# A fused matmul, tanh and multiply: pair blocks with 7 products replaced by triple blocks with 15

## The chip, the cores and the metric

The kernel runs on one core of one Trainium2 chip. The metric is device microseconds (us) for one execution, lower is better. The core has five engines that run their own instruction streams and meet through semaphores: TensorE (PE, matmuls; PEld is its weight load), VectorE (DVE), ScalarE (ACT), GpSimd (POOL) and SyncE (SP), which here only issues DMAs. Matmul results land in PSUM, eight banks of 128 partitions by 512 float32 numbers; all other on-chip data lie in SBUF.

## The reference

```python
x:  16 x 512 x 1024   float32, normal numbers
w1: 1024 x 768, w2: 1024 x 768   float32, normal numbers
y1 = np.matmul(x, w1)
y2 = np.matmul(x, w2)
return (np.tanh(y1) * y2).astype(np.float32)
```

Flattened, x is 8192 rows, that is 64 row tiles of 128 rows. The contraction length is 1024, eight blocks of 128. The output is 8192 by 768.

## The kernel before

**Head.** The first six row tiles (HEAD = 6) are computed plainly, in bfloat16, while the weights still arrive: x and the weights are loaded by SP (`load_head_x`, `load_w`), cast on DVE and ACT (`cast_wb`, L254 and L256), x is transposed on PE (`pe_transpose_f` L223 for tiles 0 to 3, `pe_transpose_b` L238 for tiles 4 and 5), and `head_mm` multiplies: 512 columns wide (L267) and 256 wide (L270), eight contraction blocks each, for both weights. `head_tanh` (L283) and `head_mul` (L287) finish, `head_store` stores. Meanwhile the sums of absolute values of the weights (`abs_w` L260), `sum_w_all` (L300) and `powers` (L347 to L350) give a power of two for each weight, with which DVE and ACT make scaled float16 blocks `b11`, `b21`, `b22` (`cast_w`) and their differences `t1` to `t4` (`t_block`, L318 and L322).

**Steady part.** The other 58 row tiles go in 29 pairs. A pair of tiles (two block rows) by the two halves of the contraction, against the two halves of the contraction by the two halves of a weight's columns, is a 2x2 by 2x2 block product, done with 7 block products in place of 8 by the scheme that the names s1 to s4, t1 to t4 and p1 to p7 spell out. A *unit* is one pair with one weight: 7 products, each four matmuls of 384 columns (`product`, L401). The combinations after the products are made in part by accumulating several products in one PSUM bank, in part by ACT copies (`op_seed` L414 seeds a bank with another's contents, `copy_out` L418), in part by DVE additions (`add_out` L423). For w1 the unit ends with tanh on ACT with a scale (L431), for w2 with a multiplication on DVE (`final`, L437) into the output tile, which SP stores (L452).

**Operands of x.** For each pair: SP loads two tiles (L334), ACT sums absolute values (L340), DVE takes powers of two (L347 to L350), DVE or ACT casts with the reciprocal to float16 (L360, L362), SP transposes by DMA (L368), DVE makes four operand sums of 128x512 (L382), and `out_scales` (L390) prepares the factors that undo the scaling.

**Order.** The first ten units and the head follow ORDER, four lists written out (PE, ACT, DVE, DMA); `schedule` gives them times with cost figures and emits them in that order. Later units follow a fixed slot table: seven slots of 0.65 us a unit, with a due slot for each step (`unit_ops`). Products stand in the slots -6 p1, -3 p5, -2 p2, 0 p6, 2 p3, 3 p7, 6 p4. The steps on ACT and DVE that hand a bank on lie between: p7 (slot 3), then the DVE addition c22, then p4 (slot 6). Neighbouring units overlap and fill each other's gaps. GpSimd issues nothing in the steady part; it does four small steps for the last two units (L442, L448).

**The end.** The last multiplication on DVE covers 384 columns, and its store 192 KB; the other halves of the last tiles were stored earlier.

Of the kernel before, what the change touches and what calls it, by code (L numbers as in the profile page):

```python
# [8 lines left out]
ACT = mybir.ActivationFunctionType  # L9
ALU = mybir.AluOpType  # L10


@with_exitstack
def kernel(
# [15 lines left out]

    nc = tc.nc
# [3 lines left out]
    BM = B * M  # L35
    KO = K // P
    KH = KO // 2
    MT = BM // P
    Q = N // 2
    F = 512  # L40
    G = N - F
    HEAD = 6
    WARM = 21
    PAIRS = (MT - HEAD) // 2
    FIRST = 6
    PLANNED = 10
    T_BUFS = 2
    O_BUFS = 4
    LOADS = ("x0 a0 x1 a1 x2 a2 x3 a3 a4 a5 a6 a7 b0 b1 b2 b3 b4 b5 b6 b7").split()
    ABS = ((1, 1, 1, 1, 1, 1, 1, 1), (2, 0, 2, 0, 2, 0, 1, 1))  # L50
    GATE = {4: 2, 5: 4, 6: 6, 7: 7}
    BLOCKS = ({"b11": ("dve", 20), "t1": ("dve", 22), "b22": ("act", 23), "t2": ("dve", 25), "b21": ("act", 25),
               "t3": ("dve", 28), "t4": ("dve", 30)},
              {"b11": ("act", 42), "t1": ("dve", 44), "b22": ("act", 46), "t2": ("dve", 48), "b21": ("act", 45),
               "t3": ("dve", 50), "t4": ("dve", 52)})
    EARLY = ("La0", "La1", "La2", "La3")

    ELSEWHERE = {
        "e01": "dve", "e11": "dve", "e20": "act", "e21": "dve", "e31": "dve", "ca0": "act", "ca1": "act",
        "cb4": "act", "b22a": "dve", "cx11": "act", "cx31": "act", "cx61": "act"  # L60
    }
    FILL = {"m00F0": 3, "m00F1": 6}
    ORDER = {
        "pe": """
            T00 T01 m00F0 m00G0 T10 T11 m00F1 m00G1 m10F0 T20 m10G0 m10G1 m10F1 T21 m20G0 m20F0 m20F1 m20G1
            m10G2 m20G2 m00F2 m00G2 m20F2 m10F2 T30 T31 m10G3 m00G3 m20F3 m10F3 m20G3 m00F3 m10F4 m10G4 m20F4
            m20G4 m00G4 m00F4 m30G0 m30G1 m30G2 m30G3 m20G5 m10G5 m10F5 m20F5 m20G6 m10G6 m10F6 m30G4 m30G5
            m30G6 m20G7 m10G7 m30G7 m10F7 m00F5 m00F6 m00F7 suma m11F0 m20F6 m20F7 m01F0 m00G5 m00G6 m00G7
            m11F1 m01F1 m30F0 m30F1 m30F2 m30F3 m30F4 m30F5 m30F6 m30F7 m21F0 m21F1 m11F2 m21F2 m01F2 m11F3
            m21F3 m01F3 m31F0 m31F1 m31F2 m31F3 m21G0 m21G1 m21G2 m21G3 m31G0 m31G1 m31G2 m31G3 m01F4 m31G4  # L70
            m21G4 m11F4 m01G0 m01G1 m11G0 m11G1 m01G2 m01G3 m01G4 m31F4 T4 m11F5 m11F6 m01F5 m31F5 m01G5 m01G6
            m31F6 m01F6 m31G5 m31G6 m01F7 m31F7 m11F7 m31G7 T5 m40F0 m40F1 m40F2 m40F3 m40F4 m40F5 m40F6 m01G7
            m40F7 m21G5 m21G6 m50F0 m50F1 m50F2 m50F3 m50F4 m50F5 m50F6 m50F7 m21F4 m21F5 m21G7 m21F6 m21F7
            m11G2 m11G3 m11G4 m11G5 m11G6 m11G7 m40G0 m50G0 m50G1 m50G2 m50G3 m50G4 m50G5 m50G6 m50G7 m40G1
            m40G2 m40G3 m40G4 m40G5 m40G6 m40G7 sumb m41F0 m41F1 m41F2 m41F3 m41F4 m41F5 m41F6 m41F7 m41G0
            m41G1 m41G2 m41G3 m41G4 m41G5 m41G6 m51G0 m51G1 m51G2 m51G3 m51G4 m51G5 m51G6 m51G7 m41G7 m51F0
            m51F1 m51F2 m51F3 m51F4 m51F5 m51F6 m51F7 p1.0 p1.1 p5.0 p6.0 p2.0 p3.0 p7.0 p5.1 p6.1 p4.0 p2.1
            p7.1 p1.2 p3.1 p4.1 p1.3 p6.2 p2.2 p5.2 p6.3 p2.3 p5.3 p7.2 p7.3 p3.2 p4.2 p3.3 p4.3 p1.4 p1.5
            p5.4 p5.5 p2.4 p6.4 p6.5 p2.5 p7.4 p7.5 p3.4 p3.5 p4.4 p4.5 p1.6 p1.7 p5.6 p6.6 p2.6 p6.7 p2.7
            p7.6 p3.6 p5.7 p7.7 p4.6 p3.7 p1.8 p4.7 p1.9 p2.8 p6.8 p5.8 p5.9 p7.8 p1.10 p3.8 p4.8 p3.9 p6.9  # L80
            p2.9 p2.10 p7.9 p5.10 p4.9
        """,
        "act": """
            ca0 absa0 ca1 absa1 e20 absa2 absa3 absa4 absa5 absa6 absa7 tanh2G absb0 tanh1F tanh0G tanh2F cb4
            tanh0F absb2 absb6 tanh3F absb4 ax00 absb7 ax01 b21a tanh4F tanh5F ax10 ax11 tanh4G ax20 cx11 b11b
            b22b seed.0 seed.1 s5.0 u2.0 ax21 b21b u2.1 f00.0 s5.1 f10.0 ax31 seed.2 ax30 seed.3 f11.0 u2.2
            u2.3 s5.2 s5.3 f00.2 f01.0 ax40 cx31 f10.2 seed.4 ax41 seed.5 s5.4 s5.5 u2.4 u2.5 f11.2 f00.4 ax51
            f01.2 ax50 f10.4 seed.6 f11.4 seed.7 f01.4 u2.6 s5.6 ax61 u2.7 s5.7 f00.6 f11.6 f10.6 seed.8 ax60
            f00.8 u2.8 f01.6 s5.8 cx61 s5.9 seed.9 f10.8 seed.10 u2.9 f01.8 f11.8 f00.10 s5.10
        """,  # L90
        "dve": """
            e00 e01 e10 e11 ca2 e21 ca3 ca4 e30 ca5 ca6 e31 ca7 parta cb0 cb1 scalea b11a cb2 cb3 t1a b22a hx4
            cb6 cb5 t2a e41 cb7 hx5 mul0F mul3F mul1F e51 t3a rx0 cx00 cx01 mul2G mul2F mul0G partb t4a rx1
            cx10 scaleb mul4F sx0 mul4G s1.0 s2.0 s4.0 s3.0 sx1 t1b t2b t3b c22.0 rx2 sx2 cx20 t4b s1.1 c22.1
            f00.1 s2.1 c12.0 f10.1 s3.1 cx21 c12.1 s4.1 f11.1 rx3 cx30 c22.2 c22.3 s3.2 s1.2 f00.3 f01.1 c12.2
            c12.3 s2.2 f10.3 mul5F rx4 cx40 s4.2 cx41 s3.3 c22.4 f11.3 c22.5 f00.5 s1.3 c12.4 f01.3 s2.3 f10.5
            rx5 f11.5 s4.3 cx50 c12.5 f01.5 c22.6 sx3 cx51 c22.7 f00.7 s1.4 s2.4 sx4 s3.4 c12.6 c12.7 rx6 cx60
            s4.4 sx5 f01.7 c22.8 f10.7 f11.7 s1.5 s2.5 c12.8 s3.5 c12.9 f00.9 c22.9 s4.5 f11.9 f01.9 f10.9
        """,
        "dma": """  # L100
            Lx0 La0 Lx1 La1 Lx2 La2 Lx3 La3 La4 La5 La6 La7 Lb0 Lb1 Lb2 Lb3 Lb4 Lx4 Lb5 Lb6 Lx5 Lb7 Lp00 Lp01
            Lp10 Lp11 Tx00 Lp20 Tx01 st3 Lp21 Tx10 Lp30 st4 Tx11 Lp31 st1 Tx20 Lp40 Lp41 Tx21 st2 Lp50 Tx30
            Lp51 Tx31 Lp60 st5 Tx40 Lp61 st0 Tx41 Lp70 store1.5 Tx50 store0.5 Lp71 Tx51 store0.1 store1.1 Tx60
            store0.7 store1.7 Tx61 store1.3 store0.3 store0.9 store1.9
        """,
    }
    LATENCY = {"pe": 0.2, "act": 0.12, "dve": 0.12, "dma": 1.4, "pool": 1.4, "none": 0.0}

    bf16 = mybir.dt.bfloat16
    f16 = mybir.dt.float16  # L110
    f32 = mybir.dt.float32
    i32 = mybir.dt.int32
# [5 lines left out]
    pool = lambda name, bufs: ctx.enter_context(tc.tile_pool(name=name, bufs=bufs))  # L118
    once = pool("once", 1)
    xfpool = pool("xf", 6)  # L120
    xhpool = pool("xh", 4)
    xtpool = pool("xt", 10)
    spool = pool("s", 3)
    smpool = pool("sm", 8)
    hopool = pool("ho", HEAD // 2)
    pspool = ctx.enter_context(tc.tile_pool(name="ps", bufs=1, space=bass.MemoryType.PSUM))
    banks = [pspool.tile([P, 512], f32, name=f"bank{i}") for i in range(8)]

    pin = tc.keep_in_program_order

    head_stack, opool = ExitStack(), []
    head = head_stack.enter_context(tc.tile_pool(name="head", bufs=1))
    w1_stack = ExitStack()
    w1_pool = w1_stack.enter_context(tc.tile_pool(name="w1f", bufs=1, side="right"))
    w_f = [p.tile([P, KO, N], f32, name=f"wf{t}") for t, p in enumerate((w1_pool, head))]
    w_b = [[head.tile([P, N], bf16, name=f"wb{t}{k}") for k in range(KO)] for t in range(2)]
    asum_w = [once.tile([P, sum(n > 0 for n in ABS[t])], f32, name=f"asum_w{t}") for t in range(2)]
    junk = once.tile([P, 2 * N], bf16, name="junk")  # L140
    ones = once.tile([P, P], f32, name="ones")
    ident = once.tile([P, P], f32, name="ident")
    ident_b = once.tile([P, P], bf16, name="ident_b")

    wt = [{n: once.tile([P, KH, Q], f16, name=f"{n}_{t}")
           for n in ("b11", "b21", "b22", "t1", "t2", "t3", "t4")}
          for t in range(2)]

    def feed(n, bank=banks[3]):
        for _ in range(n):
            pin(nc.tensor.matmul(bank[:, :2 * P], ones.bitcast(bf16)[:, :P], ones.bitcast(bf16), start=True, stop=True))

    pin(nc.vector.memset(ones, 2.0 ** -12))
    feed(WARM, banks[7])
    make_identity(nc, ident)
    pin(nc.vector.tensor_copy(ident_b, ident))

    events = []

    def at(time, fn, *args):
        events.append((time, len(events), fn, args))

    def emit():
        for _, _, fn, args in sorted(events, key=lambda e: e[:2]):
            fn(*args)
        events.clear()  # L170

    plan = {}

    def op(name, engine, cost, due, needs, fn, *args):
        plan[name] = (engine, cost, [n for n in needs if n], fn, args)
# [576 lines left out]
```

## Time and profile before

The runs took 316.24 to 316.66 us, median 316.66. The profiled execution has a span of 314.2 us from the first to the last instruction; so 2.46 us lie between this span and the median, outside the instructions that the profile shows.

| From the profile before | Value |
|---|---|
| Span of the profiled execution, beside the median | 314.2 us, 316.66 us |
| Granted PE clock | 1.000 |
| First matmul that is not a warm-up, first product of a unit, last product | 6.2, 43.9, ends about 310.5 us |
| HBM read, written | 39.85 MB, 25.17 MB |
| DMA queue of SP and ACT, share of 16 engines | 88.0% |
| x loads: count, size, issue to landing | 64, 512 KB, 5.8 us |
| DMA transposes: count, issue to landing | 58, 3.7 us |
| Stores of 384 KB: count, issue to landing | 62, 3.6 us |
| Stores of 192 KB from SP: count, issue to landing | 3, 1.9 us |

The profile's lines name the kernel's line, the engine, the operation, the tile written and those read, the shape and the number of instructions. "Busy" is the time in which an engine executed something. The chain of waits follows the work that ended last back to what released it, step by step, so it tells which engine the end depends on. A stretch's row lists each engine's busy time in it.

### The profile page before, as it was taken

How to read it: one execution, taken by the hardware profiler on the slowest of the kernel's cores; microseconds unless marked ns; L12 is line 12 of the kernel's file. 1: busy time of each engine (PE TensorE's matmuls, PEld its weight loads, DVE VectorE, ACT ScalarE, POOL GpSimd, SP SyncE). 2: the span in 40 equal slices, each digit the busy share in tenths (PEclk: the TensorE clock that was granted, in tenths of full speed). 3: DMA queues.
4: the chain of work that ended last, by engine and by line, in shares of the span. 5: the costliest groups of instructions: out<-in, count | busy, mean ns of one | idle time of the engine just before them, and what ended most of it. 6: DMA issues, size and time to landing. Idle time of an engine off the chain costs nothing.

```text
span 314.2 us, 5489 instructions
## 1 busy us (share of the span) xinstructions
PE 307.3 (98%) x1893; PEld 185.6 (59%) x1898; DVE 244.8 (78%) x571; ACT 230.5 (73%) x453; POOL 4.3 (1%) x10
## 2 busy tenths in 40 slices
PE   7999999999999999999999999999999999999995
PEld 5756656666656555555555556555555555555662
DVE  1688988888788778877777887777788777778653
ACT  3798879787888777778777777877777787776552
POOL 0000000000000000000000000000000000000004
PEclk9999999999999999999999999999999999999999
DMA  7999398999999999999999989999998989985322
GB/s 276 407 399 381 78 310 237 271 299 258 290 288 310 297 272 231 228 294 266 285 240 252 273 253 225 291 252 259 253 251 281 260 256 271 237 256 126 144 103 100
DMA packets 82300, 80.59 MB, mean 256 GB/s; under 512 B 63584, under 2 KB 64096, under 8 KB 82272
## 3 DMA queue, kind: packets, MB, share of 16 engines
q1 hardware_dynamic: 81552, 78.46, 88.0%
q10 hardware_dynamic: 720, 1.77, 1.4%
q8 instruction: 15, 0.25, 0.3%
q14 instruction: 13, 0.11, 0.1%
HBM read 39.85 MB, written 25.17 MB: 207 GB/s over the span
## 4 chain that ended last, share of the span: by engine, by line
PE 89%; DMA 8%; DVE 1%; issue 1%; ACT 0%; ACTq 0%; SPq 0%; DVEq 0%
PE bank L401 84%; DMA wf<-in_w_dram 8%; PE bank L267 3%; PE bank L270 2%; DVE t L318 1%; DVE s L382 1%; PE bank L238 0%; DVE o L437 0%; ACT o L283 0%; ACTq L250 0%; SPq L250 0%; ACT junk L260 0%; PE bank L300 0%; DVE o L287 0%; DVE out_r L390 0%
## 5 line engine op out<-in xcount | busy, mean ns | idle before, releaser
L401 PE MATMUL bank<-t,s 128*128 128x384 f16 x696 | 131.5, 326 | 0.4 <-DVE t L318 0.4
L401 PEld LDWEIGHTS <-s 128*128 128x128 f16 x928 | 90.7, 98 | 61.1 <-issue 0.8
L401 PEld LDWEIGHTS <-xT 128*128 128x128 f16 x696 | 68.0, 98 | 46.7 <-issue 0.9
L401 PE MATMUL bank<-b,xT 128*128 128x384 f16 x464 | 93.7, 326 | 0.0
L423 DVE TENSOR_TENSOR c<-bank,u 128x384 f32<-128x384 f32 x58 | 31.9, 553 | 41.1 <-PE bank L401 39.6
L340 ACT ACTIVATE junk<-x_f 128x1024 bf16<-128x1024 f32 x58 | 60.8, 1049 | 2.4 <-DMA x_f<-in_x_dram 2.4
L431 ACT ACTIVATE th<-c,out_r 128x384 f32<-128x384 f32 x58 | 35.3, 609 | 21.1 <-DVE c L423 21.1
L401 PE MATMUL bank<-b,s 128*128 128x384 f16 x232 | 47.0, 326 | 0.0
L401 PE MATMUL bank<-t,xT 128*128 128x384 f16 x232 | 46.9, 325 | 0.0
L418 ACT ACTIVATE u<-bank 128x384 f32<-128x384 f32 x58 | 28.2, 487 | 20.0 <-PE bank L401 19.7
L360 DVE TENSOR_SCALAR x_h<-x_f,pr 128x1024 f16<-128x1024 f32 x55 | 41.0, 746 | 0.2
L431 ACT ACTIVATE th<-bank,out_r 128x384 f32<-128x384 f32 x58 | 33.3, 574 | 6.1 <-PE bank L401 6.1
L414 ACT ACTIVATE bank<-bank 128x384 f32<-128x384 f32 x58 | 27.9, 481 | 12.6 <-DVE o L437 10.0
L437 DVE SCALAR_TENSOR_TENSOR o<-bank,out_r,th 128x384 f32<-128x384 f32 x58 | 35.4, 610 | 2.0 <-PE bank L401 2.0
L423 DVE TENSOR_TENSOR c<-bank,s 128x384 f32<-128x384 f32 x58 | 32.1, 554 | 6.1 <-PE bank L401 5.0
L437 DVE SCALAR_TENSOR_TENSOR o<-c,out_r,th 128x384 f32<-128x384 f32 (+1 forms) x57 | 34.3, 606 | 0.4 <-ACT th L431 0.2
L418 ACT ACTIVATE s<-bank 128x384 f32<-128x384 f32 x58 | 27.9, 482 | 7.3 <-PE bank L401 5.1
L382 DVE TENSOR_TENSOR s<-xT 128x512 f16<-128x512 f16 x58 | 24.0, 416 | 0.2
L267 PE MATMUL bank<-wb,xTb 128*128 128x512 bf16 x91 | 23.6, 379 | 0.1
L270 PE MATMUL bank<-wb,xTb 128*128 128x256 bf16 x96 | 14.6, 273 | 0.1
L260 ACT ACTIVATE junk<-wf 128x768 bf16<-128x768 f32 (+1 forms) x13 | 12.8, 988 | 1.4 <-DMA wf<-in_w_dram 1.2
L267 PEld LDWEIGHTS <-xTb 128*128 128x128 bf16 x96 | 9.3, 99 | 7.5 <-DVE xTb L231 0.3
(49 smaller groups left out, 143.4 us busy)
## 6 DMA issues: line engine op xcount, KB each, us to landing
x_f<-in_x_dram SPq DMA_DIRECT2D x64, 512.0 KB, 5.8
out_dram<-o SPq DMA_DIRECT2D x62, 384.0 KB, 3.6
wf<-in_w_dram SPq DMA_DIRECT2D x12, 384.0 KB, 7.7
wf<-in_w_dram ACTq DMA_DIRECT2D x4, 384.0 KB, 8.5
xT<-x_h SPq DMA_TRANSPOSE x58, 3.7
out_dram<-o SPq DMA_DIRECT2D x3, 192.0 KB, 1.9
out_dram<-o ACTq DMA_DIRECT2D x1, 192.0 KB, 1.9
```

Of the source, the lines that this page charges most:

```text
L260: pin(nc.scalar.activation(junk[:, :n * N].rearrange("p (k n) -> p k n", n=N), w_f[t][:, k:k + n, :], ACT.Abs, accum_out=asum_w[t][:, j:j ...
L267: pin(nc.tensor.matmul(bank, hx[mt][:, k, :], w_b[t][k][:, :F], start=k == 0, stop=k == KO - 1))
L270: pin(nc.tensor.matmul(bank[:, at_:at_ + G], hx[mt][:, k, :], w_b[t][k][:, F:], start=k == 0 and mt % 2 == 0, stop=k == KO - 1, skip_group ...
L340: pin(nc.scalar.activation(junk[:, :K], xs[HEAD + 2 * i + h], ACT.Abs, scale=2.0 ** -12, accum_out=pair_sum[i][:, h:h + 1]))
L360: pin(nc.vector.tensor_scalar(xh, xs.pop(mt), pair_r[i][:, h:h + 1], None, ALU.mult))
L382: pin((nc.vector if eng == "dve" else nc.gpsimd).tensor_tensor(s, st[i, a], st[i, b], op))
L401: pin(nc.tensor.matmul(bank[:, cols], st[i, a][:, k, :], wt[t][b][:, k, cols], start=start and k == 0, stop=stop and k == KH - 1, skip_gro ...
L414: pin(nc.scalar.activation(ub[u]["b"][:, :Q], ub[u]["a"][:, :Q], ACT.Copy))
L418: pin(nc.scalar.activation(c, ub[u][bank][:, :Q], ACT.Copy))
L423: pin(nc.vector.tensor_tensor(c, ub[u][bank][:, :Q], ub[u][other], ALU.add))
L431: pin(nc.scalar.activation(th, v, ACT.Tanh, scale=rs[i][:, 0, h:h + 1]))
L437: pin(nc.vector.scalar_tensor_tensor(o[:, h, q * Q + cols.start:q * Q + cols.stop], v, rs[i][:, 1, h:h + 1], tanhs[i, h, q][:, cols], ALU. ...
```

## The change

The head stays at six plain tiles, one plain tile is added at the end (TAIL = 1), and the other 57 go in 19 triples. In a triple, three row tiles by the two halves of the contraction meet two halves of the contraction by three column groups: columns 0 to 511 of w1, columns 0 to 511 of w2, and the last 256 columns of both weights side by side. Each group is 512 columns wide. The plain way takes 3 x 2 x 3 = 18 block products; the new scheme takes 15, p0 to p14, each four matmuls of 512 columns. Both weights are so done in one unit.

What it asks for beside the products: 11 sums of weight blocks, once (B_SUMS, DVE, 128x2048 float16 each); 10 sums of x blocks in each triple (A_SUMS, 128x512, on DVE or GpSimd); and in each triple 7 copies from PSUM on ACT ("copy", "seed"), 8 additions on DVE ("add"), three tanh and three multiplications of 512 columns ("t", "m") and of 256 ("th", "mh").

Operands are cast to float16 without scaling. The loads of tiles 4 to 63 convert from float32 in the DMA, issued from GpSimd; the transposes of these tiles are DMAs from SP. ACT still sums the absolute values of every x tile and of each of the 16 weight slices (`aw`), but nothing waits for them before the end. There, DVE and one matmul count how many of the sums lie between 512 and 1024 and write a flag; all engines load it into a register, and if a sum was outside, a branch takes `general_path`, which computes everything again with scaled operands, tile by tile.

The order of all engines' work is made by a class `Planner` when the kernel is built. It takes each step's needs, cost and due time, walks forward in time and gives each step to the engine, among those allowed, that can start it first. The order of the products is fixed by PE_ORDER, in which "+" marks products of the triple before. Its 15 positions give this table for one triple (in slots of one product): p10 0, p7 2, p6 4, p9 5, p12 7, p8 8, p11 10, p3 11, p4 16, p2 18, p13 21, p5 24, p1 27, p0 28, p14 29. PSUM banks are also given out by the planner.

```diff
-    HEAD = 6
-    PAIRS = (MT - HEAD) // 2
+    HEAD = 6
+    TAIL = 1
+    TRIPLES = (MT - HEAD - TAIL) // 3
+    LOW, HIGH = 512.0, 1024.0
+    XH_BUFS, XT_BUFS, S_BUFS, O_BUFS, C_BUFS, WF_BUFS = 5, 10, 2, 3, 2, 8
...
+A_SUMS = (
+    (5, 1, 4, "add"), (13, 5, 8, "add"), (20, 16, 4, "sub"), (12, 4, 8, "add"), (28, 12, 16, "sub"),
+    (15, 2, 13, "add"), (60, 32, 28, "sub"), (47, 15, 32, "sub"), (42, 47, 5, "sub"), (63, 16, 47, "sub"),
+)
+B_SUMS = (
+    (48, 32, 16, "sub"), (40, 8, 32, "sub"), (3, 1, 2, "sub"), (6, 2, 4, "sub"), (43, 3, 40, "sub"),
+    (44, 4, 40, "add"), (45, 6, 43, "add"), (18, 16, 2, "sub"), (19, 1, 18, "add"), (36, 44, 8, "sub"),
+    (27, 8, 19, "sub"),
+)
...
+C_OPS = (
+    ("p10", "p", (), "c0", 32, 8, True),
+    ("copy327", "copy", ("p10",), "s327", "c0", 1),
+    ("p6", "p", (), "c1", 15, 40, True),
+    ("add263", "add", ("copy327", "p6"), "c2", "c1", "s327", (-1, 1)),
+    ("p12", "p", ("add263",), "c2", 47, 44, False),
+    ("seed7", "seed", ("p12",), "c3", "c2", -1),
+    ("p11", "p", ("seed7",), "c3", 42, 36, False),
+    ("copy7", "copy", ("p11",), "s7", "c3", -1),
+    ("p7", "p", (), "c4", 16, 1, True),
+    ("p4", "p", (), "c6", 12, 3, True),
+    ("add64", "add", ("copy327", "p7"), "s64", "c4", "s327", (1, 1)),
+    ("t2", "t", ("add64",), 2, "s64", 1),
+    ("p14", "p", ("p12", "seed7"), "c2", 63, 4, False),
+    ("th2", "th", ("p14",), 2, "c2", 1),
+    ("mh2", "mh", ("p14", "th2"), 2, "c2", 1),
+    ("p9", "p", ("add64", "p7"), "c4", 28, 19, False),
+    ("copy191", "copy", ("p9",), "s191", "c4", 1),
+    ("p8", "p", ("copy191", "p9"), "c4", 20, 18, False),
+    ("copy63", "copy", ("p8",), "s63", "c4", -1),
+    ("p3", "p", ("copy63", "p8"), "c4", 8, 27, False),
...
+)
+
+PE_ORDER = "10 4+ 7 2+ 6 9 13+ 12 8 5+ 11 3 1+ 0+ 14+"
...
+class Planner:
+    LATENCY = {"pe": 0.25, "act": 0.15, "dve": 0.15, "pool": 0.2, "sp": 1.6, "cast": 2.2}
...
-    def product(i, t, n, bank, start, stop, cols=slice(0, Q)):
-        a, b = PRODUCTS[n]
-        for k in range(KH):
-            pin(nc.tensor.matmul(bank[:, cols], st[i, a][:, k, :], wt[t][b][:, k, cols],
-                                 start=start and k == 0, stop=stop and k == KH - 1,
-                                 skip_group_check=True))
+    def product(e, i, dst, a, b, begins):
+        for k in range(KH):
+            pin(nc.tensor.matmul(place(i, dst), x_operand(i, a)[:, k, :], w_rhs(b, k),
+                                 start=begins and k == 0, stop=k == KH - 1, skip_group_check=True))
...
-    def load_x(mt):
-        t = xfpool.tile([P, K], f32, tag="xf", name="x_f")
-        pin(nc.sync.dma_start(t, xf[mt]))
-        xs[mt] = t
+    def load_x(e, mt):
+        xhs[mt] = xhpool.tile([P, K], f16, tag="xh", name="xh")
+        pin(nc.gpsimd.dma_start(xhs[mt], xf[mt]))
...
+    def x_sum(e, i, v, a, b, how):
+        ss[i, v] = spool.tile([P, KH, P], f16, tag=f"s{v}", name=f"s{v}")
+        pin(engine[e].tensor_tensor(ss[i, v], x_operand(i, a), x_operand(i, b), OP[how]))
...
+            op(f"S{v}.{i}", {"dve": 0.416, "pool": 1.2}, None, x_needs(i, a) + x_needs(i, b), x_sum, i, v, a, b, how,
+               behind=[f"{r}.{i - S_BUFS}" for r in a_readers[v]] if i >= S_BUFS else [])
...
+        op(f"L{mt}", {"pool": 0.55}, None, [], load_x, mt,
+           issued=[prev] + ([f"T{mt - AHEAD}"] if mt - AHEAD >= 4 else []), behind=([f"T{j + 4}", f"D{j + 4}"] if j >= 0 else []), xfer=1.38)
+        op(f"T{mt}", {"sp": 0.05}, None, [f"L{mt}"], transpose, mt,
+           behind=xt_readers[mt - XT_BUFS] if mt >= XT_BUFS else [], xfer=1.2)
+        op(f"D{mt}", {"act": 1.25}, ORIGIN - 12 + 4.33 * (mt - HEAD), [f"L{mt}"], abs_x, mt)
...
+    plan.backward({"S": 3.0, "T": 4.0, "L": 6.0, "B": 3.0})
+    order = plan.run()
...
+    flag = nc.values_load(bad[:1, :1], min_val=0, max_val=1)
+    with tc.If(flag > 0, preferred_fallthrough_block=False):
+        general_path(tc, xf, wr, of, N, F)
```

## The prediction

> **What bounds the kernel now.** I read the page's busy rows first, then the chain of waits, then the table of stretches over the steady part, then the timeline of one row pair, and the DMA rows last.
>
> The page's busy rows give the share of the span and the number of instructions; the chain is the same page's part 4.
>
> ```profile
> PE 307.3 (98%) x1893; PEld 185.6 (59%) x1898; DVE 244.8 (78%) x571; ACT 230.5 (73%) x453; POOL 4.3 (1%) x10
> ...
> PE 89%; DMA 8%; DVE 1%; issue 1%; ACT 0%; ACTq 0%; SPq 0%; DVEq 0%
> ```
>
> From the chain of waits in order of time (start, length, what):
>
> ```profile
> 1.15 7.63 DMA wf<-in_w_dram
> ...
> 44.83 1.77 DVE t L318
> 46.60 0.03 issue
> 46.63 263.86 PE bank L401 x1612
> 310.49 0.03 issue
> ...
> 310.58 0.62 DVE o L437
> ```
>
> So from 46.63 to 310.49 us nothing but the unit matmuls of L401 sets the end: 263.86/1612 = 163.7 ns for each 384-column matmul. A busy PE alone would prove little, but here the chain never leaves PE. Whoever wants to win must give PE fewer columns; the other engines must only keep up. The stretches of the steady part (length, then busy time of PE, PEld, DVE, ACT, POOL, clock, DMA share, GB/s) show how much room they have:
>
> ```profile
> 144.10:153.20 9.10, 9.10 (x58) 5.41 (x57) 7.38 (x18) 6.80 (x15) 0.00 (x0) 1.00 1.07 289
> 153.20:162.30 9.10, 9.10 (x57) 5.46 (x56) 7.38 (x18) 6.80 (x15) 0.00 (x0) 1.00 0.91 264
> ```
>
> 9.10 us is one pair of row tiles, 4.55 us a tile; DVE is at 81%, ACT at 75%, GpSimd idle, the clock full, and the DMA engines near 100%. The timeline tells what a back-to-back instruction really costs:
>
> ```profile
> 147.79 0.61 DVE L437 SCALAR_TENSOR_TENSOR o<-c,out_r,th 128x384 f32<-128x384 f32 x1
> ...
> 148.32 0.61 DVE L437 SCALAR_TENSOR_TENSOR o<-bank,out_r,th 128x384 f32<-128x384 f32 x1
> ...
> 151.32 0.60 ACT L431 ACTIVATE th<-c,out_r 128x384 f32<-128x384 f32 x1
> ...
> 151.82 1.04 ACT L340 ACTIVATE junk<-x_f 128x1024 bf16<-128x1024 f32 x1
> ...
> 152.86 0.56 ACT L431 ACTIVATE th<-bank,out_r 128x384 f32<-128x384 f32 x1
> ```
>
> Starts lie 0.53 us apart for a 0.61 us DVE instruction, 0.50 for a 0.60 us ACT one, and the absolute sum with its accumulator read takes 1.04 from start to start. Durations overlap their neighbours by some 0.08 us on DVE and 0.10 on ACT, so sums of durations overstate the load.
>
> **What the Trainium skill says.** "TensorE: Matmul & The Clock Gate", Back-to-back issue gap: a warm matmul of N columns follows the last by N/2.4 + 2.5 ns, 162.5 for 384 and 215.8 for 512. This trace agrees: 163.7 with all small stalls, and three 512-column matmuls in the chain take 0.65 us. "SBUF — State Buffer", Who interferes with whom: a DVE instruction with two SBUF inputs and a GpSimd instruction that reads SBUF exclude each other for their whole length; one SBUF input does not. No run here shows it, since GpSimd idles until 305 us. "DMA: Bandwidth & Descriptors", SWDGE vs HWDGE vs iDMA: a converting DMA can only be issued by GpSimd, which writes the descriptors itself; this trace has none. "Runtime: NRT & Kernel Launch", Instruction fetch mechanics: a taken branch outside the fetched window waits for its page; this trace has none.
>
> **The change, part by part.** The sum is made against the profiled span of 314.2 us; the median of the runs is 316.66, so 2.46 us lie around it and are taken as unchanged.
>
> 1. *Matmuls of the block part.* Before: 29 pairs x 2 weights x 7 products x 4 = 1624 matmuls of 384 columns. After: 19 triples x 15 x 4 = 1140 of 512, and one plain tile at the end with 3 x 8 = 24 of 512. Bare: 1624 x 0.1625 = 263.9; 1164 x 0.216 = 251.4. Measured before is 1624 x 0.1637 = 265.8, so 0.7% are stalls; the same share after gives 253.2. Change: -12.6. It lies wholly on the path.
>
> 2. *Head on PE.* Tiles 0 to 5 keep their columns. The 16 PE transposes of tiles 4 and 5 go (chain rows 0.45 and 0.45), as do the two scale sums (0.12 in the chain): -1.0. PE's first work still waits for x and the first w blocks, unchanged.
>
> 3. *Head on DVE.* Scales, b and t blocks go; 11 weight sums come. A 1536-element f16 sum took 0.952, a 512-element one 0.416, so 2048 elements cost 0.952 + 512 x 0.000523 = 1.22; 11 make 13.4 us. From 20 to 44 us DVE was nearly full before. With casts of w2 (up to 8 x 0.56), six tiles' multiplications (6 x 1.1) and the first triple's sums, about 29 us of work stand in some 24. But PE_ORDER needs the weight sums spread over the first 24 slots of 0.86 us, and the head's plain matmuls can be put between. If that cover is gone, PE waits: 0 to 6 us; I take +1.0. Lower bound 0, as nothing here feeds PE sooner. Tiles 4 and 5 now come by a converting load and a DMA transpose behind the third w2 load; head matmuls of tiles 0 to 3 (20.8 us) hide that.
>
> 4. *Steady part, DVE.* For a triple: 8 combinations and 3 multiplications of 512 at 0.68 (the head's 128x512 multiplication took 682 ns), 3 of 256 at about 0.42, 10 operand sums at 0.416: 12.9 us of durations in 15 x 0.864 = 12.96 us. With 24 overlaps of 0.08 it is 11.0, or 85%, even with nothing on GpSimd. The multiplication by pr (0.746 a tile), the powers of two and out_r (0.65 a pair) are gone; that is what pays. *ACT*: 7 copies at 0.59 (481 ns plus 128 columns), 3 tanh at 0.59 and 3 at about 0.38, 3 absolute sums at 1.04: 10.2, less 13 overlaps of 0.10: 8.9 us, 69%; 16 weight sums at 1.03 add 0.87 a triple. *Waits*: every hand-over that a product waits for (p7 to p9, p9 to p8, p8 to p3, p6 to p12, p12 to p11, p5 to p1) has two other products between, 1.73 us, for one 0.6 to 0.7 us instruction and some 0.4 of signalling. About 0.65 us is left for whatever is queued ahead. Before, p7 to p4 had 1.3 us for a 0.55 us instruction and PE did not stop. I take +0.5 over the run; 0 to 20 is possible, priced below.
>
> 5. *GpSimd and SP.* The 58 later loads leave SP for GpSimd; conversion rides on them, so the DVE cast between load and transpose goes and SP's transposes wait for the load alone. Operand sums that the planner puts on GpSimd queue with the loads there, and a load waiting for a free buffer holds the sums behind it; a late sum holds a product. SP keeps the transposes and stores in one queue, where a late transpose delays a store, which 3 buffers per row position cover. Costed at 0.
>
> 6. *End.* After the last product came one 0.62 us multiplication and a 192 KB store, 1.9 us to landing. Now: a tanh (0.4), a multiplication (0.4), and a 384 KB store, about 0.5 us longer at the head's 400 GB/s: +1.5 with one more hand-over. Then the flag is read into registers and a branch skips the general path. The reading waits only for a matmul made earlier, so it can lie under the last store; the branch and its meeting of engines can not. Nothing in the trace prices it; the nearest thing is the end after the last landing, about 1 us. Bounds 0 and 6; I take two such meetings, +2.2.
>
> Sum: -12.6 - 1.0 + 1.0 + 0.5 + 1.5 + 2.2 = -8.4. Span 305.8, median 308.3.
>
> **The rivals.** *B, the ends eat the gain.* Head stall 5, exit 4 beyond the store: -12.6 - 1.0 + 5 + 0.5 + 1.5 + 4 = -2.6, 314.1 us. For it: DVE's full head. Against: sums may be late by 20 us.
>
> *C, slower: DVE and GpSimd share the read of SBUF.* GpSimd took 0.994 us for 384 elements of two inputs and 0.703 for 192, so 512 take 1.19. A DVE operand sum that meets one waits up to 1.19 us, and the combination queued behind it has 0.65 to spare: PE stalls 0.54. One such meeting per triple costs 19 x 0.54 = 10.3, giving 318.6. It decides from 8.4/19 = 0.44 us a triple on. For it: planned orders put sums on both engines, and the planner's code models no shared port. Against: the load of point 4, which lets DVE run ahead of a plan that counts full durations, and the 3 us margin that operand sums are given.
>
> *E, the DMA engines bind.* From 135 to 235 us their share is 96.7% with 22 to 23 tiles, 4.3 us a tile, against a new period of 12.96/3 = 4.32. If converting loads cost 0.15 more than plain ones the period is 4.45: 57 x 0.13 = 7.4 lost, 315.7. Against: the share counts packets stretched by each other (a 4096-byte packet's median is 159 ns, its mean 190), and half as many bytes are written.
>
> *D, the fast path is not enough.* If a sum of absolute values left 512 to 1024, the general path would run and add hundreds of us. For normal data a row of 1024 sums to 817 with a deviation of 19, so it is excluded but for an error: 1%.
>
> **How the numbers follow.** Forecast (303.5 to 312.5): 58%. B: 13%. E: 10%, half of it faster, 1% equal, 4% slower. C: 16%. D: 1%. The remaining 2% lie within 0.2% of before, about what a measurement of this kernel can tell from no change. Faster 0.76, same 0.03, slower 0.21. The range runs from 303.5, where head and exit cost nothing beyond the longer store, to 319.5, which takes in C's one meeting per triple.
>
> **What would show it.** Right: L-lines of product matmuls x1140 at about 216 ns spacing, chain over 85% PE, 12.96 to 13.1 us a triple, DVE and ACT below 90%. The first triple starting more than 2 us after the head's matmuls run out, or PE idle before 45 us, shows point 3 low; more than 7 us from the last matmul to the end shows point 6 low. Periods over 13.4 us with DVE operand sums longer than 0.416 and GpSimd busy beside them show C; PE waiting for xT behind DMA shows E. The forecast fails if any of these together passes 8.4 us.

## The result and the profile after

The changed kernel took 337.47 us in the median of four runs (334.03 to 339.59), the kernel before 316.45 (316.02 to 316.66). The ratio is 1.063, with an interval of 1.058 to 1.069: 6% slower, where 308.3 us had been forecast, 2.6% faster. Executions of some variants below lie up to 15 us apart: a median here is over all of them, a ratio over the undisturbed ones only, and a trace is of one execution, whose time is given where it matters.

The profiled execution (339.59 us) has a span of 337.8 us, 23.6 more than before. The page's busy rows, the row of the granted clock and the DMA queues:

```profile
PE 299.8 (89%) x1394; PEld 138.1 (41%) x1394; DVE 246.9 (73%) x407; ACT 216.3 (64%) x430; POOL 149.2 (44%) x161
...
PEclk9999996997999999999999999999999999999998
...
q1 hardware_dynamic: 74880, 47.72, 58.1%
q0 software_dynamic: 8640, 15.73, 30.5%
```

PE executes 500 matmuls fewer and is no longer at 98%. GpSimd, idle before, is at 44%. The clock row has gaps for the first time. The second DMA line is the new queue: 8640 packets of GpSimd's converting loads, 30.5% of the 16 engines' span for 15.73 MB. The chain of waits, which carried the argument before, lists nothing in this profile, so the waits are read next (engine, line, what it waited for: us in total, times, longest):

```profile
POOL s L380 <- PE bank L421: 87.5, 30, 5.7
...
PE bank L421 <- DVE bank L436: 18.9, 19, 2.2
...
DVE s L380 <- DMA xT<-xh: 16.2, 8, 3.2
```

The first row is the longest, but it is not on the path: GpSimd waits for a buffer to come free, and the view has no row in which PE waits for GpSimd. The second is on the path: products wait for additions on DVE. The third is DVE waiting for transposes. The stretches (columns as before) show three kinds of triple:

```profile
44.00:57.00 13.00, 7.92 (x27) 3.03 (x26) 10.55 (x12) 5.36 (x11) 8.39 (x10) 0.74 1.07 268
95.80:108.80 13.00, 13.00 (x62) 5.87 (x61) 10.53 (x20) 11.22 (x24) 7.50 (x9) 1.00 1.03 213
264.10:277.10 13.00, 10.03 (x47) 4.39 (x46) 8.93 (x16) 6.96 (x15) 7.09 (x8) 1.00 0.92 175
```

In the middle row PE is busy throughout: such a triple takes 12.95 us from p10 to p10, as against 12.96 predicted. In the first row DVE looks busy with 10.55 us, but for only 12 instructions; in the last PE is short of 3 us and no other engine is above 9. Neither row has an engine at its limit.

I measured the gaps ahead of each product in the trace as the distance from the preceding matmul's start less 0.217 us. They sum to 31.4 us: 12.2 ahead of p12, 10.5 ahead of p5, 8.3 ahead of p9, 0.4 ahead of the twelve others. With them the span is accounted for:

| Part of the span | Predicted | Measured |
|---|---|---|
| Start to the first product | 43.9 - 1.0 + 1.0 = 43.9 | 42.9 |
| Matmuls from there, at 0.216 us | 253.2 (with small stalls) | 1173 x 0.216 = 253.4 |
| Stalls of PE ahead of products | 0.5 | 31.4 |
| Clock below full speed | 0 | 3.2 (what is left over) |
| Start of the last matmul to the end | 3.9 + 3.7 = 7.6 | 6.9 |
| Sum | 305.2 | 337.8 |

The predicted parts come to 0.6 us less than the span on record, 305.8, since the small stalls around before's first products (2.7 us for twelve matmuls that take 2.0 without them) are in none of them. The matmul saving of 12.6 us is there, and the stalls cost two and a half times as much. They have two causes.

**DVE is held while GpSimd reads.** The timeline from 73 us, DVE, GpSimd and PE together in order of start (start, length, engine, what; a count over 1 joins neighbours):

```profile
73.44 4.79 DVE L444 TENSOR_TENSOR o<-o,s 128x256 f32<-128x256 f32 x1
73.46 1.17 POOL L380 TENSOR_TENSOR s<-xT,s 128x512 f16<-128x512 f16 x1
74.58 2.26 POOL L380 TENSOR_TENSOR s<-xT 128x512 f16<-128x512 f16 x2
...
76.80 1.14 POOL L380 TENSOR_TENSOR s<-s,xT 128x512 f16<-128x512 f16 x1
...
78.15 0.68 DVE L436 TENSOR_TENSOR bank<-s,bank 128x512 f32<-128x512 f32 x1
78.75 1.27 DVE L436 TENSOR_TENSOR s<-bank,s 128x512 f32<-128x512 f32 x2
...
79.48 1.57 PE L421 MATMUL bank<-b,s 128*128 128x512 f16 x4 [2.90 <-DVE s L436]
```

A multiplication that takes 0.42 us elsewhere takes 4.79: it starts with the first of four GpSimd sums and ends 0.29 us after the last. Behind it in DVE's queue stands add64, and PE waits 2.9 us for that one with p9. This stall (3.07 us as a gap) and one of 5.25, behind an operand sum held for 4.59 us at 44.80, make up all that p9 lost.

What p5 lost has another form, the same in eleven triples (0.94 or 0.95 us each). One of them, in the same kind of view:

```profile
147.02 0.43 DVE L380 TENSOR_TENSOR s<-xT 128x512 f16<-128x512 f16 x1 [0.87 <-DMA xT<-xh]
147.07 2.50 POOL L380 TENSOR_TENSOR s<-xT 128x512 f16<-128x512 f16 x2 [3.07 <-PE bank L421]
...
148.56 1.56 DVE L444 TENSOR_TENSOR o<-o,s 128x512 f32<-128x512 f32 x1
149.53 1.60 POOL L380 TENSOR_TENSOR s<-s,xT 128x512 f16<-128x512 f16 x1
...
151.38 0.38 PE L421 MATMUL bank<-b,s 128*128 128x512 f16 x1 [0.79 <-DVE bank L436]
```

The multiplication takes 1.56 us in place of 0.68. It starts 0.14 us into the second of the two GpSimd sums at 147.07 and ends 0.55 us after that one, so here DVE did get its turn between two GpSimd sums, and the next GpSimd sum is the longer one, 1.60 us in place of 1.15. In all eleven triples DVE had just stood for a late xT, here 0.87 us, elsewhere up to 3.15 (each time a transpose landed some 0.08 us before DVE went on). So the hold fell on PE whole: p5 waits for add38, which is queued behind this multiplication.

The groups (count | busy us, mean ns of one | idle before) show the same over the run:

```profile
L380 POOL TENSOR_TENSOR s<-xT,s 128x512 f16<-128x512 f16 x37 | 43.0, 1164 | 64.1 <-PE bank L421 61.9 <-DVE s L380 1.9
...
L444 DVE TENSOR_TENSOR o<-o,bank 128x512 f32<-128x512 f32 x38 | 25.9, 681 | 11.3 <-PE bank L421 11.2
...
L444 DVE TENSOR_TENSOR o<-o,s 128x512 f32<-128x512 f32 x19 | 22.8, 1200 | 0.0
...
L380 DVE TENSOR_TENSOR s<-xT 128x512 f16<-128x512 f16 x22 | 16.4, 747 | 21.2 <-DMA xT<-xh 16.2 <-PE bank L421 4.7
```

A 512-column multiplication takes 681 ns with one input from PSUM and, in the mean, 1200 with both from SBUF. The combinations, with one SBUF input, stay at 674 to 687. Against 685, 415 and 420 ns without a hold, the multiplications lose 19 x 0.515 + 19 x 0.252 and the three longer groups of operand sums 22 x 0.327 + 38 x 0.116 + 20 x 0.046: 27 us of DVE time. The planner put 94 of the 190 operand sums on GpSimd. That a DVE instruction with two SBUF inputs contends with a GpSimd instruction that reads SBUF is what the Trainium skill states in "SBUF — State Buffer", Who interferes with whom; the trace agrees. A hold through several GpSimd instructions is not stated there.

**Transposes come late.** The timeline of DVE around 190 us:

```profile
189.07 0.69 DVE L436 TENSOR_TENSOR s<-bank,s 128x512 f32<-128x512 f32 x1 [0.24 <-PE bank L421]
192.41 0.43 DVE L380 TENSOR_TENSOR s<-xT 128x512 f16<-128x512 f16 x1 [2.64 <-DMA xT<-xh]
192.75 0.68 DVE L436 TENSOR_TENSOR s<-bank,s 128x512 f32<-128x512 f32 x1
193.35 0.69 DVE L436 TENSOR_TENSOR bank<-s,bank 128x512 f32<-128x512 f32 x1
```

DVE stands before an operand sum whose xT has not landed; add263 (193.35) is queued behind it, and p12 starts at 194.09, 1.8 us late. The DMA rows (KB each, us from issue to landing) show transposes at 5.8 us, which took 3.7 before:

```profile
xh<-in_x_dram POOLq DMA_DIRECT2D x60, 256.0 KB, 5.6
...
xT<-xh SPq DMA_TRANSPOSE x60, 5.8
```

### The profile page after: what moved, and what is told of

Its sections match the earlier page's. It is cut to its first block, busy times and chain, and to the rows that moved or that the text cites. A ratio compares the mean times of both kernels' runs of the same rounds, so it can differ in the third digit from the quotient of the medians.

```text
span 337.8 us, 4563 instructions
## 1 busy us (share of the span) xinstructions
PE 299.8 (89%) x1394; PEld 138.1 (41%) x1394; DVE 246.9 (73%) x407; ACT 216.3 (64%) x430; POOL 149.2 (44%) x161
## 3 DMA queue, kind: packets, MB, share of 16 engines
q0 software_dynamic: 8640, 15.73, 30.5%
## 4 chain that ended last, share of the span: by engine, by line
## 5 line engine op out<-in xcount | busy, mean ns | idle before, releaser
L421 PE MATMUL bank<-b,s 128*128 128x512 f16 x608 | 144.8, 382 | 26.9 <-DVE bank L436 18.9
L380 POOL TENSOR_TENSOR s<-xT,s 128x512 f16<-128x512 f16 x37 | 43.0, 1164 | 64.1 <-PE bank L421 61.9
L380 POOL TENSOR_TENSOR s<-xT 128x512 f16<-128x512 f16 x35 | 42.3, 1226 | 53.6 <-DMA xT<-xh 28.0
L336 ACT ACTIVATE junk<-xh 128x1024 f16<-128x1024 f16 x60 | 63.1, 1052 | 0.9 <-DMA xh<-in_x_dram 0.7
L427 ACT ACTIVATE s<-bank 128x512 f32<-128x512 f32 x95 | 55.9, 589 | 9.5 <-PE bank L421 9.5
L436 DVE TENSOR_TENSOR bank<-s,bank 128x512 f32<-128x512 f32 x76 | 52.2, 687 | 4.3 <-PE bank L421 3.6
L444 DVE TENSOR_TENSOR o<-o,bank 128x512 f32<-128x512 f32 (+1 forms) x76 | 40.3, 548 | 17.6 <-PE bank L421 11.2
L421 PE MATMUL bank<-b,xT 128*128 128x512 f16 x228 | 52.5, 379 | 0.0
L394 PE MATMUL bank<-wh,xT 128*128 128x512 f16 (+1 forms) x200 | 39.3, 353 | 1.3 <-DVE wh L312 0.7
L421 PE MATMUL bank<-wh,s 128*128 128x512 f16 x152 | 39.9, 386 | 0.0
L380 DVE TENSOR_TENSOR s<-s,xT 128x512 f16<-128x512 f16 x38 | 20.4, 536 | 11.8 <-PE bank L421 10.4
```

Of the source, the lines that this page charges most:

```text
L336: pin(nc.scalar.activation(junk[:, :src.shape[-1]], src, ACT.Abs, scale=scale, accum_out=sums[:, column:column + 1]))
L380: pin(engine[e].tensor_tensor(ss[i, v], x_operand(i, a), x_operand(i, b), OP[how]))
L394: pin(nc.tensor.matmul(b, xts[mt][:, k, :], rhs, start=first, stop=k == KO - 1, skip_group_check=True))
L421: pin(nc.tensor.matmul(place(i, dst), x_operand(i, a)[:, k, :], w_rhs(b, k), start=begins and k == 0, stop=k == KH - 1, skip_group_check=T ...
L427: pin(nc.scalar.activation(d, place(i, src), ACT.Copy, scale=float(sign)))
L436: pin(nc.vector.tensor_tensor(d, a, b, ALU.add if signs == (1, 1) else ALU.subtract))
```

## The experiments

Two theories stood against each other: the hold of DVE by GpSimd's sums, and DMA that delivers too late. All kernels ran beside the kernel before, whose median was 315.95 to 316.18 us in these runs. Gaps are those ahead of the products, as above.

**1. All operand sums on DVE** (the planner orders anew):

```diff
-  op(f"S{v}.{i}", {"dve": 0.416, "pool": 1.2}, ...
+  op(f"S{v}.{i}", {"dve": 0.416}, ...
```

> All ten operand sums of a triple on DVE, none on GpSimd; the planner orders anew. Theory 1 (DVE instructions with two SBUF inputs are held while GpSimd reads SBUF): the multiplications o<-o,s and the sums on DVE return to 0.68 and 0.42 us, the PE gaps before p9 (8.3 us) and p5 (10.5 us) go, 315 to 322 us. Theory 2 (the DMA engines deliver x too late): the gaps before p12 (12.2 us) stay or grow, and the time stays above 325. Theory 3 (DVE has no room: 12.9 us of durations in 12.96): gaps appear before products that wait for additions in every triple, 330 us or more.

Measured: median 320.52 us (311.74 to 326.56), ratio 0.995 (0.991 to 0.999). In the trace (321.65 us) the gaps fell from 31.4 to 14.7: p5 from 10.5 to 1.7, p9 from 8.3 to 0.9, p12 stayed at 11.5. The groups:

```profile
L380 DVE TENSOR_TENSOR s<-xT 128x512 f16<-128x512 f16 x57 | 24.0, 421 | 16.5 <-DMA xT<-xh 14.5 <-PE bank L421 1.1
...
L444 DVE TENSOR_TENSOR o<-o,s 128x512 f32<-128x512 f32 x19 | 13.0, 685 | 0.0
```

No DVE group is longer than its unhindered time, though DVE now does twice the sums. By the ratios (1.0633 less 0.9948, of 316 us) 21.6 us come back, by the medians 17.0. What is left is the wait for xT (14.5 us), so a second cause exists.

**2. GpSimd writes in place of adding.** The order and the engines stay as changed; this kernel leaves the GpSimd sums out and fills their results with zeros, so GpSimd reads no SBUF for them, does not wait for x, and is quicker (528 ns each in place of some 1160).

```diff
-  pin(engine[e].tensor_tensor(ss[i, v], x_operand(i, a), x_operand(i, b), OP[how]))
+  if e == "pool":
+      pin(nc.gpsimd.memset(ss[i, v], 0.0))
+  else:
+      pin(engine[e].tensor_tensor(ss[i, v], x_operand(i, a), x_operand(i, b), OP[how]))
```

> Same plan and order as the changed kernel, but each operand sum on GpSimd is a memset of its result, so that these sums are left out: GpSimd writes SBUF and reads none, and doesn't wait for x. Theory 1: DVE durations return to 0.68 and 0.42, gaps before p9 and p5 go, 318 to 324 us, with the p12 gaps of some 12 us left. Theory 2: p9 and p5 gaps are DVE sums waiting for x; little changes, above 330 us.

Measured: 311.74 to 323.91 us, median 315.17. In the trace, of the quickest execution, the gaps are 6.3 us, 5.4 of them ahead of p12.2 and p12.3 (p12 of the third and fourth triple), and every later triple takes 12.95 to 13.25. The group:

```profile
L447 DVE TENSOR_TENSOR o<-o,s 128x512 f32<-128x512 f32 x19 | 13.0, 685 | 0.0
```

With DVE's order untouched, 22.3 us come back by the medians. The reading GpSimd sums were the price, not the number of instructions on DVE. How much of it is the hold and how much GpSimd's shorter work this run does not separate; DVE's durations alone are the hold's. Some 12 us of gaps ahead of p12 had been expected to stay; 5.7 did.

**3 and 4. A third of the stores' bytes**, which leaves 512 of the 768 output columns of these tiles unwritten; once with the sums as changed, once with all on DVE:

```diff
-  pin(nc.sync.dma_start(of[mt], out_tile(mt)))
+  pin(nc.sync.dma_start(of[mt][:, :G], out_tile(mt)[:, :G]))
```

> Same plan, but each store writes 256 of 768 columns, the rest of the output is left unwritten: 0.65 us less DMA engine time a tile. Theory 1: the gaps before p9 and p5 stay (19 us), the gaps before p12 shrink at most; 325 to 332 us. Theory 2: DMA share falls below 0.9, x arrives in time, gaps before p12 and part of the rest go, 315 to 323 us.

> Both at once: sums on DVE alone, and stores of 256 columns, the rest of the output left unwritten. If theories 1 and 2 each own their gaps, nearly all 31 us of gaps go and the time is 305 to 310 us. If DVE is too full (theory 3) it stays over 318 whatever the DMA does.

| | stores whole | stores cut |
|---|---|---|
| Sums on DVE and GpSimd | 337.47, ratio 1.063, gaps 31.4 | 326.32, ratio 1.032 (1.029 to 1.036), gaps 27.4 |
| All sums on DVE | 320.52, ratio 0.995, gaps 14.7 | 307.58, ratio 0.962 (0.957 to 0.967), gaps 7.4 |

By the ratios, lighter DMA gives 9.8 us with the hold and 10.4 without; taking the hold away gives 21.6 and 22.3 (by the medians 11.1, 12.9, 17.0 and 18.7). As times the two causes add up within the intervals, and neither hides the other. Of what the cut stores give, 2.5 and 2.9 us are the shorter way from the last matmul to the end (4.4 and 3.9 us in place of 6.9) and no lateness of x. With cut stores and the hold in place the p5 and p9 gaps stay (9.8 and 7.9 us). In a single stall the causes meet: in one triple of experiment 3 DVE had waited only 0.1 us for xT when the same hold of 0.88 us came, and p5 lost 0.24 us in place of 0.95. The last cell's median lies 0.7 us under the forecast of 308.3; part of that is chance, since 7.4 us of gaps remain and the cut stores also shorten the end.

**5 to 7. More loads in flight**, all sums on DVE, to let transposes come sooner; then the same without weight casts on GpSimd; then the first with cut stores:

```diff
-  XH_BUFS, XT_BUFS, S_BUFS, O_BUFS, C_BUFS, WF_BUFS = 5, 10, 2, 3, 2, 8
+  XH_BUFS, XT_BUFS, S_BUFS, O_BUFS, C_BUFS, WF_BUFS = 8, 12, 2, 3, 2, 8
-  AHEAD = 3
+  AHEAD = 5
```

In the second also:

```diff
-  op(f"c{a}{k}", {"dve": 0.56, "act": 0.83, "pool": 2.3} if t else {"dve": 0.56, "act": 0.83}, ...
+  op(f"c{a}{k}", {"dve": 0.56, "act": 0.83}, ...
```

> All sums on DVE as in sums_dve, and more buffers for x: 8 in place of 5 for the loaded tile, 12 in place of 10 for the transposed one, loads up to 5 in place of 3 tiles ahead of the transposes. If x comes late because its pipeline is short (theory 2a: the DMA engines have the capacity on average), the gaps before p12 shrink from 11.5 us to under 5, the runs scatter less, and the time is 306 to 313 us. If the DMA engines are simply full at this pace (theory 2b), the gaps only move, DMA share stays near 1.2, and the time stays at 315 to 325.

> As deep, and the weight casts are not allowed on GpSimd, so that the first converting loads no longer stand behind a cast there (28.3 us in the changed kernel). Theory 2a: x is ahead when the first triples start, the gaps before p12.2 and p12.3 (some 5 us in sums_dve) go, 2 to 5 us faster than deep. Theory 2b: early loads take DMA time from the last weights, the same time or up to 3 us slower.

> As deep, with stores of 256 columns, the rest of the output left unwritten. Both theories: 302 to 308 us, about the sum of its matmuls. Theory 2a: only 2 to 5 us below deep; theory 2b: over 8 us below deep.

Measured: 328.29 us, ratio 1.029 (1.026 to 1.032); 324.14, ratio 1.017 (1.012 to 1.021); 316.71, ratio 0.996 (0.994 to 0.999). The remedy makes it worse: the first lies above both ranges that had been given for it, the third above the 302 to 308 of both theories. In the first (trace: 336.16 us), p10 of the first triple comes at 50.1 us where it was 42.9, and of 22.6 us of gaps 17 stand ahead of p10 and p8 in place of p12. Its DMA row:

```profile
xT<-xh SPq DMA_TRANSPOSE x60, 8.8
```

With more in flight the transposes landed later than the 6.8 us of experiment 1 (their packets took 35.3 ns in the mean and not 31.1), so the lateness moved and grew. Without GpSimd's weight casts it is 4 us less, with ranges that overlap, and p12 of the third triple still waits 4.0 us; with cut stores it is 11.6 us less. Depth was not what lacked.

**8. No absolute sums of x.** All sums on DVE, and the absolute sums of the 60 tiles that are loaded by GpSimd are left out, so a load's buffer waits for the transpose alone and ACT has 1.05 us less a tile.

```diff
-  behind=([f"T{j + 4}", f"D{j + 4}"] if j >= 0 else [])
+  behind=([f"T{j + 4}"] if j >= 0 else [])
...
-  op(f"D{mt}", {"act": 1.25}, ..., abs_x, mt)
```

> As sums_dve, with the absolute sums of the 60 later x tiles left out (their check is left out, the weights' stays): 3.1 us less ACT a triple, DMA as before. A control for sp_loads. ACT has room, so if DMA is the remaining limit: 312 to 324 us as in sums_dve. If ACT's queue holds copies back: 3 or more us faster.

Measured: median 312.56 us (308.13 to 321.62), ratio 0.989 (0.986 to 0.991), gaps 9.0. That is 8 us under experiment 1 by the medians and 2 by the ratios, on another chip and with ranges that overlap; the transposes land after 6.2 us against 6.8, still far from 3.7. So this work is not the cause of their lateness.

**9. Plain loads from SP.** As 8, the same sums left out, but x comes as float32 through SP's queue, in four buffers, and ACT casts it (into three buffers, where the converting loads had five):

```diff
-  pin(nc.gpsimd.dma_start(xhs[mt], xf[mt]))
+  pin(nc.sync.dma_start(xss[mt], xf[mt]))
...
+  pin(nc.scalar.copy(xhs[mt], xss[mt]))
```

> As no_abs (the check of x left out), but x is loaded as float32 by SP, in the queue of the transposes and stores, and cast on ACT, 1.1 us a tile; GpSimd does nothing. Theory 2c (converting loads on a queue of their own interleave with the transposes and stretch them): DMA share in the steady part falls from 1.2 to about 1.0, transposes land in about 4 us, the gaps before p12 go, 303 to 309 us, and the runs agree within 1%. Theory 2d (any loads at this pace fill the DMA engines): share stays near 1.2, 312 us or more.

```profile
xs<-in_x_dram SPq DMA_DIRECT2D x60, 512.0 KB, 5.5
...
xT<-xh SPq DMA_TRANSPOSE x60, 3.7
```

The DMA rows are what was to be shown: with twice the bytes written to SBUF, transposes land after 3.7 us, as before the change, the engines' share from 83 us on falls to 0.87 to 0.98 (1.07 to 1.25 up to 252 us in experiment 1), and SP needs 1.42 us to issue a transpose where it needed 2.71. The slower pace is not the reason (13.7 us a triple and not 12.95): in experiment 13, at up to 17.4 us a triple and with converting loads, transposes still land after 5.7. So it is the converting loads on GpSimd's queue that make the transposes late. The time did not follow: median 322.56 us, ratio 1.019 (1.016 to 1.022), gaps of 20.4 us now spread over p8, p10, p12 and p11. PE waits 6.3 us for ACT, in whose queue the casts of 1.04 us now stand, 3.9 us for DVE and 3.8 us for the first xT; that the casts are behind the first two is likely and not shown. A plain load from GpSimd's queue was not tried, so conversion and queue are not told apart.

**10 to 12. Loads less far ahead**, all sums on DVE, then both kernels again on another chip:

```diff
-  AHEAD = 3
+  AHEAD = 2
```

> As sums_dve, but a converting load goes out only when the transpose two tiles before has been issued, not three: fewer loads in flight beside the transposes. Theory 2c (loads on GpSimd's queue crowd out the transposes): transposes land sooner than the 6.8 us of sums_dve, the gaps before p12 shrink, the runs scatter less, 308 to 315 us. Against it: if the loads' own latency then sets the pace, a period cannot be under 3/2 of a load's time to landing plus the wait for the transpose's issue, and the time rises over 322 us.

> sums_dve once more, on the same chip as ahead2_again. If loads three tiles ahead cost time, 314 to 324 us with a scatter of several us as the first time; if the first time was that chip, 309 to 313 us, as ahead2.

> ahead2 once more: 308.5 to 312.5 us if its gain over sums_dve was not the chip's. The step from three to two tiles ahead is then worth the difference to sums_dve_again.

Measured: median 310.43 us (308.69 to 312.34), ratio 0.982 (0.979 to 0.985), and the gaps fell to 6.1 us. On the other chip 314.49 us (306.62 to 319.70), ratio 0.975 (0.971 to 0.980), beside 317.47 (311.27 to 319.57) for AHEAD = 3. Two stretches of the first run:

```profile
122.00:148.00 26.00, 26.00 (x122) 11.82 (x121) 22.96 (x50) 19.47 (x39) 3.18 (x6) 1.00 1.06 210
70.00:83.00 13.00, 10.32 (x41) 4.17 (x40) 7.83 (x17) 8.57 (x19) 1.06 (x2) 0.87 1.25 201
```

The upper one is two triples with PE never idle, and DVE, with all sums on it, busy for 88% of the time. The lower one, where the DMA share is 1.25, holds the one large stall left (2.84 us ahead of p12). This kernel computes all that the changed one does and is the quickest such version that I ran. That the load distance is the reason is not shown: its transposes land after 7.2 us, no sooner than the 6.8 of experiment 1, and on one chip the two differ by 3.0 us with ranges that overlap.

**13. Load distance alone**: the same edit of AHEAD, with the line of the sums as the change has it:

> The changed kernel with nothing but loads two tiles ahead in place of three; operand sums stay on DVE and GpSimd. Theory 1 as the larger cause: DVE instructions with two SBUF inputs stay long, gaps before p9 and p5 stay near 19 us, 326 to 334 us. If the load distance alone were the cause: 315 us or less.

Measured: 375.34 us (373.29 to 376.88), ratio 1.188 (1.182 to 1.194), far above both ranges that had been given. The group:

```profile
L444 DVE TENSOR_TENSOR o<-o,s 128x512 f32<-128x512 f32 x19 | 55.9, 2940 | 0.0
```

The planner's new order puts 106 sums on GpSimd, three in a row just when the last 512-column multiplication comes. It takes 2.94 us in the mean, and 4.2 us in twelve triples, in which it is held through all three. Then add38 behind it is late and p5 waits 2.8 us (34.2 of 53.5 us of gaps). From the sixth triple on one takes 15.8 to 17.4 us. Another 15 us of the span, estimated as what is left when matmuls, gaps, a wait of 1.9 us ahead of the flag's matmul and both ends are taken off, go to spells of half the clock (granted mean 0.936). Beside the same loads with all sums on DVE on the same chip (ratio 0.975) the GpSimd sums cost 67 us, where they cost 21.6 with AHEAD = 3. One constant, far from the sums in the code, made them three times as dear.

## Why the prediction was wrong

**Point 1, matmuls -12.6: right.** 1140 products' matmuls, 216 ns apart, 12.95 us a triple where nothing waits. The section of the Trainium skill that the prediction took 215.8 ns from, "TensorE: Matmul & The Clock Gate", Back-to-back issue gap, gives this formula for the isolated matmul and about 131 ns for 512 columns in a stream; here the stream itself ran at 216, so the measurement decides.

**Points 2 and 3, the head: right within 1 us.** The first product comes 1.0 us sooner; nine head matmuls (33 plain ones lie behind it, less the last tile's 24) now stand behind it, 1.9 us, so the head cost 0.9 where 0 had been taken. Weight sums took 1.22 us each as worked out. Losses at 51 us are not the head's load: an operand sum of 0.42 us was held for 4.59.

**Point 4, steady waits +0.5: the step that failed**, together with "Costed at 0" in point 5. The load was right: with all sums on it DVE is busy for 88% and PE does not stop (experiment 10), so "85%, even with nothing on GpSimd" stands. The slack of "about 0.65 us" per hand-over fits too: where DVE was on time, a hold of 0.88 us cost p5 0.24 us (experiment 3). What was wrong is what can stand in the queue ahead of an addition. The hold was no part of the forecast; it stood in rival C and was priced there as one operand sum that meets one GpSimd sum and has the whole slack to spare, 0.54 us of stall a triple. Three terms of that were wrong:

- The list of instructions that can be held lacked the multiplications whose both inputs lie in SBUF (the last 512- and 256-column ones of each triple), just those ahead of add38 and add64.
- The slack had already gone to late transposes in the eleven triples in which the 512-column multiplication was held for 0.88 us, so p5 lost 0.95 us each time.
- A row of GpSimd sums can count in full. It did in the two longest holds, 4.79 and 4.59 us, behind which p9 lost 8.3 us.

The stall came to (10.5 + 8.3) / 19 = 0.99 us a triple ahead of p5 and p9, plus spells of a slower clock behind the longest. Removing the GpSimd sums gave 21.6 us (experiment 1); at C's "decides from" 0.44 us a triple the sign was lost from this term alone.

**Point 5, GpSimd and SP at 0: the second miss**, rival E. Its 7.4 us were for a period of 4.45 us; the packets' times add to 4.56 us a tile (transpose 1.86, load 1.70, store 1.0), but PE lost in single waits, ahead of p12, not in an even period: 12.2 us. Cut stores gave about 10 by the ratios, 2.5 to 2.9 of them at the end. E's mechanism, converting loads that cost more than plain ones, was too narrow: the transposes beside them land later as well, and SP, which needs longer to issue each (2.1 us and not 1.4), holds the stores behind.

Rivals C and E had been set against each other with a chance each. They happened together, as experiments 3 and 4 show by adding up, and ahead of p5 each made the other dearer.

**Point 6, the end +3.7: right in size (+3.0), wrong in its parts.** The timeline of the end (SP issuing the stores):

```profile
331.22 0.83 SPq L388 DMA_DIRECT2D out_dram<-o  x2
...
332.15 0.80 SPq L388 DMA_DIRECT2D out_dram<-o_last  x1
```

The last store lands at 336.86, 4.7 us after its issue and not 2.4. Three others were issued within the 1.5 us ahead of it and landed at 333.0, 334.0 and 335.0, so it came in a row behind them. Reading the flag (0.46 to 0.92 us per engine) and the branches (0.04 to 0.2) lie wholly under that landing and cost nothing, where +2.2 had been taken. The wait for a page of instructions that the Trainium skill describes in "Runtime: NRT & Kernel Launch", Instruction fetch mechanics, is not seen in these branches.

**Rivals B and D** are excluded: the head cost 0.9 us more than predicted and the end 0.7 less, and the general path did not run.

## What to carry to other kernels

Before work is moved to GpSimd, list every DVE instruction with two SBUF inputs, multiplications on outputs included, and price each as held at least to the end of the GpSimd instruction that it meets, at worst for the longest unbroken row of those that read SBUF. Then ask which hand-over stands behind it in DVE's queue, and whether its slack is still there when inputs come late. Work that fits on DVE at 85% is better left there than shared by a planner that has no term for the hold; with such a planner a change of any constant can move rows of sums under the wrong instruction. When a transfer changes its kind or queue, look at the landing times of the other transfers beside it, not at its own bytes.

## What the runs showed of the hardware that was not expected

- A held DVE instruction sometimes gets its turn between two GpSimd sums and sometimes not. In the changed kernel's trace 35 DVE instructions with two SBUF inputs were held. 33 of them show a start inside a GpSimd sum; each ended some 0.28 us (instructions that take 0.42) or 0.55 us (those that take 0.68) after that sum, and where another GpSimd sum followed at once, that one took 1.34 to 1.61 us in place of 1.15. The other two show a start ahead of the first sum of a row, by 0.02 and 0.34 us, and stayed held through all of the row, at 44.80 us also across a DMA issue of GpSimd. In experiment 13 a start 0.27 us ahead was held through three sums, twelve times.
- A start ahead does not always lose: eleven operand sums for which DVE had stood idle started 0.05 us ahead of a GpSimd sum and took their 0.43 us, and the GpSimd sum took 1.39. What decides, and whether the starts shown are the real ones, stays open.
- Writing alone does not hold: beside GpSimd's memsets DVE's two-input instructions took 685 and 424 ns.
- Transposes that ran beside converting loads from GpSimd's queue landed after 5.6 to 8.8 us, beside plain loads from SP's queue after 3.7, although the latter wrote twice the bytes. It is not the packets' own time alone: in experiment 13 a transpose's packets took 24.8 ns in the mean, before the change 25.7, and yet the transposes landed after 5.7 us and not 3.7.
- In the changed kernel the clock granted to PE fell to half for 6.8 us from 3.2 us into the gap of 5.25 us, and for 3.4 us just after the gap of 3.07; it stayed full around those of 2.35 us and less. That is no threshold: in experiment 13 nine of twelve gaps of 2.80 us brought such a spell and three did not.
- What stays open: what makes the late transposes vary so much between executions of one kernel (up to 15 us in its time), and why AHEAD = 2 does better.
